# Routing and gathering the first chunk under the second chunk's map, in front of an expert layer

## The chip, the cores and the metric

One NeuronCore of a Trainium2 chip runs the whole kernel as one program. The metric is device time in microseconds (us). TensorE (PE) multiplies, VectorE (DVE), ScalarE (ACT) and GpSimd (POOL) work elementwise, SyncE (SP) starts most loads. Each engine works off its own queue in the order in which the program issues, and waits on semaphores for the others.

## The reference

Two layers on an input of 256 rows and 1024 columns: retention and a dense SwiGLU, then a Fourier mixer and a top-2-of-8 expert SwiGLU, then a last norm. The part that matters here is the end of the Fourier mixer and the start of the experts:

```python
hn = rms_norm(h, mix_norm[1]);  h = h + fourier_mixer(hn, fnet_w_out[0])   # fft2(...).real @ w_out
hn = rms_norm(h, ffn_norm[1]);  h = h + moe_swiglu(hn, ...)
# moe_swiglu:
logits = t @ w_router                                # 256 x 8
top_val, top_idx = lax.top_k(logits, 2)
top_w = softmax(top_val)
gates = sum(one_hot(top_idx, 8) * top_w[..., None], axis=1)
for e in range(8):
    out = out + gates[:, e:e+1] * swiglu(t, w_gate[e], w_up[e], w_down[e])
```

Here t is the normed h, with gain ffn_norm[1]; each expert is 1024 to 3584 and back.

## The kernel before

**Arithmetic.** The large products run in a 32-bit format in three parts (high times high, high times low, low times high), so every operand is split: ScalarE casts the high part (L131 for weights, L253 for data), VectorE subtracts to get the low part (L132, L254). `mm3` (L248 to L250) issues the three products.

**Weights.** `Weights` keeps one list of weight blocks (items) of 1 MB for the whole kernel. Loads go through SyncE's queue (L105) into raw buffers, eleven of them and, for the experts, four more that are lent by tiles that are free then. `split` makes the high and low halves of an item in two pieces each, into one of three slots. `get()` hands out the next item and first issues the splits of up to two items ahead. Before the expert loop, `W.ahead(W.next + W.PARTS - 1)` (L950) issues the splits of the second and third item; that of the first has been issued in the stage before.

**Rows and chunks.** The 256 rows are two chunks of 128 (c). Each row block of X has two halves of 512 columns (hf).

**End of the Fourier mixer.** `out_mm` multiplies by fnet_w_out, six products for one item, chunk and half. Of the four items the first two run for both chunks. The last two, `its`, are done by `close` (L319), quarter by quarter: for chunk c and half hf both items (12 products), then `gained`, in which VectorE adds the accumulator into X (L266) and multiplies by the norm's gain `gb` into a buffer `xgs[hf]` (L267), then the sink of the quarter before.

**Routing.** The sink, `r_sink`, transposes the four 128-column blocks of the gained rows on TensorE (L812), copies them out on ScalarE (`xt`, L813), issues the router products of the quarter before (`r_mm`, L770, four blocks into `lgp[c]`), splits the gained rows into `nh` and `nl`, and sums squares. `route(c)` (L778 to L784) finds the top two of a chunk on VectorE: `o1` marks the first, `mask` both. Then TensorE counts with the matrix `upper` (strictly above the diagonal) how many earlier rows chose the same expert; the count is copied to `pos`. For chunk 1 all rows of chunk 0 are added with `ones`. `gates()` computes the softmax weights on GpSimd into `gts`.

**Gathering.** Experts are handled in pairs by `prep(e0)` (L919). Its first step, `choose`, makes selection maps `pm` on VectorE (L845): for each chunk and expert of the pair a 128 x 128 matrix that has a one where a row sits in a slot. Four steps gather: `gather` multiplies `nh` and `nl` by the maps of both chunks, eight products of 256 columns for one q (L855, L856), and splits the result into `xe`. The last step, `place`, multiplies the maps by `gts` (L872), and VectorE copies the gates and row scales of the pair to `gl` (L874). The first pair runs ahead of the expert loop, except for the last step, which `work.pop(0)()` runs in the loop of the first 512 columns behind the first item's products.

**Experts.** For each expert and each of seven blocks of 512 columns `moe_h` issues 24 gate products (12 for each of two items), ScalarE takes the silu scaled by `RS[e]`, which lies in `gl` (L1103), then `moe_h` issues 24 up products, VectorE multiplies (L1107), and the down products of the block before follow.

The whole stage is issued under `manual_schedule()`: the order of each engine's queue is that of the program text. The tiles of the routing stage lie in pools `pt` and `pc`, those of the experts in pool `pe`.

Of the kernel before, what the change touches and what calls it, by code (L numbers as in the profile page):

```python
# [12 lines left out]
OP = mybir.AluOpType  # L13
PS = bass.MemoryType.PSUM

P = 128
# [10 lines left out]
def cp(c):  # L27
    return slice(c * P, (c + 1) * P)
# [124 lines left out]
def body(nc, tc, a, out, upto=None):  # L153
    with ExitStack() as ctx:
# [75 lines left out]

        def route_consts(rw):
            nc.scalar.dma_start(rw, a["moe_router"][0].rearrange("(k p) e -> p k e", p=P))
            kw = dict(base=0, allow_small_or_imprecise_dtypes=True)
            ge.iota(iota8, pattern=[[1, NE]], channel_multiplier=0, **kw)
            ge.iota(slot, pattern=[[1, P]], channel_multiplier=0, **kw)
            ge.memset(ones, 1.0)

        def acc(i):
            return ps.tile([P, 512], F32, name=f"acc{i}", tag=f"acc{i}")

        def mm(nm="mm"):
            return ps.tile([P, 512], F32, name=nm, tag="mm", bufs=3)
# [9 lines left out]
        def split(hi, lo, src):  # L252
            se.copy(hi, src)  # L253
            ve.tensor_sub(lo, src, hi.bitcast(F32))  # L254
# [3 lines left out]
            se.activation(hi, src, AF.Copy, scale=s)  # L258
            ve.scalar_tensor_tensor(lo, src, s, hi.bitcast(F32), op0=OP.mult, op1=OP.subtract)

        def gained(c, hf, accs=None):


            x = X[:, c, HALF[hf]]
            if accs is not None:
                ve.tensor_add(x, x, accs[2 * c + hf])  # L266
            ve.tensor_mul(xgs[hf], x, gb[:, HALF[hf]])  # L267
            return xgs[hf]

# [6 lines left out]
        def sq_tile():  # L276
            return const.tile([P, 2, 2], F32, name="sq", bufs=2)

        def square(sq, c, hf, src=None):

            se.activation(scr[0], X[:, c, HALF[hf]] if src is None else src, AF.Square, scale=1.0 / 32,  # L281
                          accum_out=sq[:, c, hf:hf + 1])
# [36 lines left out]
        def close(its, accs, sink, early=None):  # L319

            left = None
            for c in range(2):
                for hf in range(2):
                    for i, (it, lh, ll) in enumerate(its):
                        out_mm(accs, it, lh, ll, c, False, i == len(its) - 1, (hf,))
                    xg = gained(c, hf, accs)
                    if early:  # L330
                        early(c, hf)
                    if left:
                        sink(*left)
                    left = (c, hf, xg)
            return lambda: sink(*left)

        def run(hooks, i):
            for f in hooks.get(i, ()):
# [270 lines left out]
        with tc.tile_pool(name="pb", bufs=1) as pb:  # L609
            pb = Aligned(pb)  # L610
            scratch(pb)
            tabr = pb.tile([P, 2, 2 * H1], F32, name="tabr")
            tabd = pb.tile([P, 2, 512], F32, name="tabd", tag="hth", bufs=2)
            accs = [acc(i) for i in range(4)]
            rst, sq = [], sq_tile()

# [23 lines left out]
            for u in range(6):  # L640
                if u:
                    f = hidden(u - 1)
                    hooks = {0: f[:1], 1: f[1:]}
                else:
                    hooks = {1: [left]}
                n = 512 if u < 5 else 256
                g = dense_h(u, hooks)
                if not u:
                    for c in range(2):
                        for hf in range(2):  # L650
                            square(sq, c, hf)
                    rst = [inv_rms(sq, c) for c in range(2)]
                    nc.scalar.dma_start(tabr, a["dft_s"].rearrange("(c p) n -> p c n", p=P))
                    nc.scalar.dma_start(tabd, a["dft_d"].rearrange("(c p) n -> p c n", p=P))
                    gain_bcast(a["mix_norm"][1])
                    route_consts(rw)
                gs = []
                for c in range(2):
                    t = pb.tile([P, 512], F32, name="gs", bufs=3)
                    se.activation(t[:, :n], g[c], AF.Silu, scale=rst[c])  # L660
                    gs.append(t)
                o = dense_h(u)
                if u == 1:
                    split(td[0], td[1], tabd)
                hms[u] = []
                for c in range(2):
                    t = pb.tile([P, 512], F32, name="hm", bufs=3)
                    ve.scalar_tensor_tensor(t[:, :n], o[c], rst[c], gs[c][:, :n], op0=OP.mult, op1=OP.mult)
                    hms[u].append(t)
                if 1 <= u < 5:  # L670
                    for s in range(2):
                        it = W.get()
                        for c in range(2):
                            out_mm(accs, it, *lhs(hT[u - 1], s), c, u == 1 and s == 0, False)
# [26 lines left out]
        with tc.tile_pool(name="pc", bufs=1) as pc:  # L701
# [61 lines left out]

            xt = [pc.tile([P, 8, P], F32, name="xt", tag="fh", bufs=2) for _ in range(2)]
            lgp = [mm("lg") for _ in range(2)]
            sq, late = sq_tile(), []

            def r_mm(c, hf):
                for k in range(4 * hf, 4 * hf + 4):
                    te.matmul(lgp[c][:, :NE], xt[c][:, k], rw[:, k], start=k == 0, stop=k == 7)  # L770
# [35 lines left out]
                ge.tensor_add(gts[:, :, :NE], gts[:, :, :NE], g2)  # L806
                ge.tensor_copy(gts[:, :, NE], rs)

            def r_sink(c, hf, xg):
                p = tr()  # L810
                for k in range(4):
                    te.transpose(p[:, cp(k)], xg[:, cp(k)], ident)  # L812
                se.copy(xt[c][:, 4 * hf:4 * hf + 4], p.rearrange("p (k t) -> p k t", k=4))  # L813
                for ch in late:
                    r_mm(*ch)
                late[:] = [(c, hf)]
                split(nh[:, c, HALF[hf]], nl[:, c, HALF[hf]], xg)
                square(sq, c, hf)

            left = close(its, accs, r_sink)  # L820
            po = mm("po")
            route(0)
            left()
            r_mm(1, 1)
            te.matmul(po[:, 0:8], upper, mask[:, 0], start=True, stop=True)
            route(1)
            ve.tensor_copy(pos[:, 0], po[:, :8])
            te.matmul(po[:, 8:16], ones, mask[:, 0], start=True, stop=False)
            te.matmul(po[:, 8:16], upper, mask[:, 1], start=False, stop=True)
            ve.tensor_copy(pos[:, 1], po[:, 8:16])  # L830
            gates()

        pt_.close()
        if upto == "C":
            return finish()


        with tc.tile_pool(name="pe", bufs=1) as pe, tc.tile_pool(name="dr", bufs=1, space=bass.MemoryType.DRAM) as dr:
            pe = Aligned(pe)
            def choose(e0):  # L840

                pm = pe.tile([P, 2, 2 * P], F32R, name="pm")
                for c in range(2):
                    for j in range(2):
                        ve.tensor_scalar(pm[:, c, cp(j)], slot, pos[:, c, e0 + j:e0 + j + 1],  # L845
                                         mask[:, c, e0 + j:e0 + j + 1], op0=OP.is_equal, op1=OP.mult)
                return pm

            def gather(pm, xe, q, o=None):

                o = o or mm("ga")
                for i in range(2):
                    ds = cp(2 * q + i)
                    for c in range(2):
                        te.matmul(o[:, i * 256:(i + 1) * 256], nh[:, c, ds], pm[:, c], start=c == 0, stop=False)  # L855
                        te.matmul(o[:, i * 256:(i + 1) * 256], nl[:, c, ds], pm[:, c], start=False, stop=c == 1)  # L856
                ov = o.rearrange("p (i j s) -> p j i s", i=2, j=2)
                split(xe[:, :, 0, 2 * q:2 * q + 2], xe[:, :, 1, 2 * q:2 * q + 2], ov)

            def place(pm, last):  # L860

                gl = pe.tile([P, 2, NE + 1], F32, name="gl", bufs=2)
# [56 lines left out]
            def prep(e0):  # L919

                st = {}

                def first():
                    st["pm"] = choose(e0)
                    st["xe"] = pe.tile([P, 2, 2, 8, P], F32R, name="xe", bufs=2)
                    for j in range(2):
                        XE[e0 + j] = st["xe"][:, j]
                yield first
                for q in range(4):
                    yield lambda q=q: gather(st["pm"], st["xe"], q, acc(q) if not e0 else None)  # L930

                def last():
                    gl = place(st["pm"], e0 + 2 == NE)
                    for j in range(2):
                        GT[e0 + j] = gl[:, j, e0 + j:e0 + j + 1]
                        RS[e0 + j] = gl[:, j, NE:]
                yield last
# [147 lines left out]
            for u in range(NU):  # L1085
# [11 lines left out]
                for s, o in enumerate(moe_h(e)):  # L1097
                    if s == 0 and u:
                        hidden_t(u - 1)
                    if s == 0 and not u:  # L1100
                        work.pop(0)()
                hm = pe.tile([P, 512], F32, name="hm")
                se.activation(hm, o, AF.Silu, scale=RS[e])  # L1103
# [95 lines left out]
```

## Time and profile before

| | |
|---|---|
| median of 3 runs | 1424.81 us (1424.56 to 1425.46) |
| profiled execution | 1424.62 us |
| its span | 1422.8 us |
| TensorE busy | 1402.2 us, 99% |
| VectorE busy | 1164.3 us, 82% |
| ScalarE busy | 968.5 us, 68% |
| GpSimd busy | 70.1 us, 5% |
| loads | 437.97 MB, 308 GB/s in the mean |

Times in the profile count from the start of the span; the execution is 1.8 us longer. Busy TensorE is not TensorE at its peak: products overlap, and the time of one in a row (0.39 us for 512 columns) is longer than the distance to the next (0.23 us). So the text goes by the starts of products, and idle time stands in brackets behind a row together with the instruction that ended it. The Fourier mixer's last products begin near 414 us, the experts at 451.41 us.

### The profile page before, as it was taken

The page shows a single profiled execution, that of the slowest core. Times are in us where ns is not written, and L with a number is a line of the kernel's source. Part 1 is how long each engine was busy: PE and PEld are TensorE (multiplying, and loading weights), DVE is VectorE, ACT ScalarE, POOL GpSimd, SP SyncE. Part 2 cuts the span into 40 slices and gives each one's busy share as a digit, 9 for nine tenths or more (in the row PEclk, how much of TensorE's full clock was granted, in tenths as well). Part 3 has the DMA queues.
Part 4 walks back from the last instruction along what each step waited for, and adds up shares of the span by engine and source line. Part 5 has one row for each costly group of instructions (what it writes and reads, how often), then busy time and mean ns, then how long its engine had stood idle before and what let it go on. Part 6 is the DMA issues. An engine that isn't in the chain of part 4 may idle for free. (4 is left out here: it accounts for less than half of the span.)

```text
span 1422.8 us, 17302 instructions
## 1 busy us (share of the span) xinstructions
PE 1402.2 (99%) x6529; PEld 1165.5 (82%) x6529; DVE 1164.3 (82%) x1201; ACT 968.5 (68%) x1118; POOL 70.1 (5%) x109
## 2 busy tenths in 40 slices
PE   8999999999999999999999999999999999999997
PEld 6888878888888888888888888888888888888786
DVE  6866666554577999989899988998898899999996
ACT  5544445444455777777877777787787778778875
POOL 8400000000001000000000000000000000001000
PEclk9999999999999999999999999999999999999999
DMA  8646549755626989999899999999999999999990
GB/s 288 214 155 201 175 142 361 263 183 183 201 101 239 385 327 331 380 350 364 319 380 393 393 353 368 359 351 393 356 395 391 354 381 370 393 373 348 396 375 30
DMA packets 186842, 437.97 MB, mean 308 GB/s; under 512 B 8176, under 2 KB 11008, under 8 KB 186752
## 3 DMA queue, kind: packets, MB, share of 16 engines
q1 hardware_dynamic: 181424, 426.27, 82.0%
q10 hardware_dynamic: 4752, 8.44, 1.6%
q0 software_dynamic: 576, 2.10, 0.4%
q8 instruction: 52, 0.85, 0.2%
q14 instruction: 38, 0.31, 0.1%
HBM read 432.06 MB, written 4.72 MB: 307 GB/s over the span
## 5 line engine op out<-in xcount | busy, mean ns | idle before, releaser
L132 DVE TENSOR_TENSOR wlo<-raw,whi 128x1024 fp32r<-128x1024 f32 (+1 forms) x789 | 923.2, 1218 | 143.8 <-ACT whi L131 140.1
L131 ACT CAST whi<-raw 128x1024 fp32r<-128x1024 f32 (+1 forms) x789 | 786.1, 1047 | 201.5 <-PE acc L250 102.7
L248 PE MATMUL mm<-whi,xe 128*128 128x512 f32 x896 | 354.9, 396 | 0.3 <-PEq L1124 0.3
L250 PE MATMUL mm<-whi,xe 128*128 128x512 f32 x896 | 349.7, 390 | 0.0
L249 PE MATMUL mm<-wlo,xe 128*128 128x512 f32 x896 | 349.3, 390 | 0.0
L249 PE MATMUL acc<-wlo,hth 128*128 128x512 f32 x528 | 205.5, 389 | 0.9 <-DVE wlo L132 0.9
L248 PE MATMUL acc<-whi,hth 128*128 128x512 f32 x528 | 205.7, 390 | 0.0
L250 PE MATMUL acc<-whi,htl 128*128 128x512 f32 x528 | 205.5, 389 | 0.0
L250 PEld LDWEIGHTS mm<-whi,xe 128*128 128x128 f32 x896 | 168.2, 188 | 36.0
L249 PEld LDWEIGHTS mm<-wlo,xe 128*128 128x128 f32 x896 | 168.5, 188 | 33.4 <-DVE wlo L132 0.3
L248 PEld LDWEIGHTS mm<-whi,xe 128*128 128x128 f32 x896 | 168.4, 188 | 33.5 <-issue 0.7
L248 PE MATMUL mm<-whi,nhi 128*128 128x512 f32 (+1 forms) x352 | 135.6, 385 | 0.0
L250 PE MATMUL mm<-whi,nlo 128*128 128x512 f32 (+1 forms) x352 | 133.9, 380 | 0.0
L249 PE MATMUL mm<-wlo,nhi 128*128 128x512 f32 (+1 forms) x352 | 133.7, 380 | 0.0
L249 PEld LDWEIGHTS acc<-wlo,hth 128*128 128x128 f32 x528 | 99.1, 188 | 21.7 <-DVE wlo L132 1.3
L250 PEld LDWEIGHTS acc<-whi,htl 128*128 128x128 f32 x528 | 99.1, 188 | 20.6
L248 PEld LDWEIGHTS acc<-whi,hth 128*128 128x128 f32 x528 | 99.2, 188 | 20.5
L253 ACT CAST hth<-tr 128x512 fp32r<-128x512 f32 (+1 forms) x67 | 38.9, 580 | 81.0 <-PE tr L294 81.0
L250 PEld LDWEIGHTS mm<-whi,nlo 128*128 128x128 f32 x352 | 66.2, 188 | 12.8
L249 PEld LDWEIGHTS mm<-wlo,nhi 128*128 128x128 f32 x352 | 66.3, 188 | 11.9
L248 PEld LDWEIGHTS mm<-whi,nhi 128*128 128x128 f32 x352 | 66.3, 188 | 11.9
L254 DVE TENSOR_TENSOR htl<-tr,hth 128x512 fp32r<-128x512 f32 (+1 forms) x67 | 45.6, 681 | 33.5 <-ACT hth L253 33.5
(288 smaller groups left out, 989.6 us busy)
## 6 DMA issues: line engine op xcount, KB each, us to landing
raw<-in_moe_w_gate SPq DMA_DIRECT2D x110, 1024.0 KB, 7.9
raw<-in_moe_w_down SPq DMA_DIRECT2D x108, 1024.0 KB, 7.8
raw<-in_moe_w_up SPq DMA_DIRECT2D x105, 1024.0 KB, 7.9
raw<-in_ret_w_in SPq DMA_DIRECT2D x23, 1024.0 KB, 5.4
raw<-in_dense_w_gate SPq DMA_DIRECT2D x11, 1024.0 KB, 5.2
raw<-in_dense_w_up SPq DMA_DIRECT2D x11, 1024.0 KB, 8.9
raw<-in_dense_w_down SPq DMA_DIRECT2D x11, 1024.0 KB, 5.8
raw<-in_ret_w_out SPq DMA_DIRECT2D x8, 1024.0 KB, 4.8
```

The costliest lines, as they stand in the source:

```text
L131: self.nc.scalar.copy(hi[sl], t[sl])
L132: self.nc.vector.tensor_sub(lo[sl], t[sl], hi[sl].bitcast(F32))
L248: te.matmul(o, lh, rh, start=first, stop=False)
L249: te.matmul(o, lh, rl, start=False, stop=False)
L250: te.matmul(o, ll, rh, start=False, stop=last)
L253: se.copy(hi, src)
L254: ve.tensor_sub(lo, src, hi.bitcast(F32))
```

## The change

The routing stage is written out in place of `close`. Chunk 0's transposes, router products, top two, positions and first maps are issued between chunk 1's map products. Transposes now read X itself: the norm's gain is multiplied into the router's weights `rw` instead, in the dense layer's fourth block (a load of the gain as 8 x 128, a transpose, a multiplication). The gathers of the first pair are issued chunk by chunk, 16 products for chunk 0 (12 behind chunk 1's last router products and 4 behind the position products) and 16 for chunk 1. The maps for them are in a tile `pm0` of the routing stage's pool, and the splits into `xe` follow in the experts' pool; the last step of the first pair makes the maps once more in the experts' pool. `warm(n)` issues n products of 512 columns that nobody reads. The step `place` of the first pair moves from behind the first 12 gate products to behind all 24. The experts' pool is opened with `reuse_waits="tile"`, so that a tile waits for those that lay in its place, and not for the whole pool before.

```diff
         def route_consts(rw):
             nc.scalar.dma_start(rw, a["moe_router"][0].rearrange("(k p) e -> p k e", p=P))
+            nc.scalar.dma_start(rg[:8], a["ffn_norm"][1].rearrange("(k p) -> k p", p=P))
...
+        def choose(pm, e0, c):
+            for j in range(2):
+                ve.tensor_scalar(pm[:, c, cp(j)], slot, pos[:, c, e0 + j:e0 + j + 1],
+                                 mask[:, c, e0 + j:e0 + j + 1], op0=OP.is_equal, op1=OP.mult)
+
+        def gather(o, pm, q, c):
+            for i in range(2):
+                ds = cp(2 * q + i)
+                te.matmul(o[:, i * 256:(i + 1) * 256], nh[:, c, ds], pm[:, c], start=not c and not i, stop=False)
+                te.matmul(o[:, i * 256:(i + 1) * 256], nl[:, c, ds], pm[:, c], start=False, stop=bool(c and i))
...
+                if u == 3:
+                    p = tr()
+                    te.transpose(p[:, :8], rg[:8], ident[:8, :8])
+                    ve.tensor_mul(rw, rw, p[:, :8, None].to_broadcast([P, 8, NE]))
...
+            def maps(c, hf, i):
+                it, lh, ll = its[i]
+                out_mm(accs, it, lh, ll, c, False, i == 1, (hf,))
+            def r_t(c, hf):
+                p = tr()
+                for k in range(4):
+                    te.transpose(p[:, cp(k)], X[:, c, cp(4 * hf + k)], ident)
+                se.copy(xt[c][:, 4 * hf:4 * hf + 4], p.rearrange("p (k t) -> p k t", k=4))
+            def hi(c, hf):
+                se.copy(nh[:, c, HALF[hf]], xgs[hf])
+            def lo(c, hf):
+                ve.tensor_sub(nl[:, c, HALF[hf]], xgs[hf], nh[:, c, HALF[hf]].bitcast(F32))
+            def warm(n):
+                o = mm("warm")
+                for _ in range(n):
+                    te.matmul(o, nh[:, 0, :P], nh[:, 0, HALF[0]], start=True, stop=True)
-            left = close(its, accs, r_sink)
-            po = mm("po")
+            for hf in range(2):
+                maps(0, hf, 0)
+                if hf:
+                    r_t(0, 0)
+                    hi(0, 0)
+                    lo(0, 0)
+                    square(sq, 0, 0)
+                maps(0, hf, 1)
+                gained(0, hf, accs)
+            maps(1, 0, 0)
+            r_t(0, 1)
+            hi(0, 1)
+            lo(0, 1)
+            square(sq, 0, 1)
+            r_mm(0, 0)
+            maps(1, 0, 1)
+            r_mm(0, 1)
+            gained(1, 0, accs)
             route(0)
-            left()
+            maps(1, 1, 0)
+            r_t(1, 0)
+            hi(1, 0)
+            square(sq, 1, 0)
+            maps(1, 1, 1)
+            x = X[:, 1, HALF[1]]
+            ve.tensor_add(x, x, accs[3])
+            po, pm = mm("po"), pt.tile([P, 2, 2 * P], F32R, name="pm0", tag="tdh")
+            te.matmul(po[:, 0:8], upper, mask[:, 0], start=True, stop=True)
+            r_mm(1, 0)
+            ve.tensor_copy(pos[:, 0], po[:, :8])
+            choose(pm, 0, 0)
+            r_t(1, 1)
+            square(sq, 1, 1)
+            ve.tensor_mul(xgs[1], x, gb[:, HALF[1]])
+            hi(1, 1)
+            lo(1, 0)
+            warm(3)
+            go = [acc(q) for q in range(4)]
             r_mm(1, 1)
-            te.matmul(po[:, 0:8], upper, mask[:, 0], start=True, stop=True)
+            for q in range(3):
+                gather(go[q], pm, q, 0)
             route(1)
-            ve.tensor_copy(pos[:, 0], po[:, :8])
-            te.matmul(po[:, 8:16], ones, mask[:, 0], start=True, stop=False)
-            te.matmul(po[:, 8:16], upper, mask[:, 1], start=False, stop=True)
-            ve.tensor_copy(pos[:, 1], po[:, 8:16])
+            po = tr()
+            te.matmul(po[:, 0:8], ones, mask[:, 0], start=True, stop=False)
+            te.matmul(po[:, 0:8], upper, mask[:, 1], start=False, stop=True)
+            gather(go[3], pm, 3, 0)
+            ve.tensor_copy(pos[:, 1], po[:, :8])
+            choose(pm, 0, 1)
             gates()
+            warm(2)
+            lo(1, 1)
+            for q in range(4):
+                gather(go[q], pm, q, 1)
...
-        with tc.tile_pool(name="pe", bufs=1) as pe, ...
+        with tc.tile_pool(name="pe", bufs=1, reuse_waits="tile") as pe, ...
...
+                def maps():
+                    st["pm"] = pe.tile([P, 2, 2 * P], F32R, name="pm")
+                    for c in range(2):
+                        choose(st["pm"], e0, c)
                 def first():
-                    st["pm"] = choose(e0)
+                    if e0:
+                        maps()
...
+                def part(q):
+                    o = mm("ga") if e0 else go[q]
+                    for c in range(2) if e0 else ():
+                        gather(o, st["pm"], q, c)
+                    ov, xe = o.rearrange("p (i j s) -> p j i s", i=2, j=2), st["xe"]
+                    split(xe[:, :, 0, 2 * q:2 * q + 2], xe[:, :, 1, 2 * q:2 * q + 2], ov)
                 for q in range(4):
-                    yield lambda q=q: gather(st["pm"], st["xe"], q, acc(q) if not e0 else None)
+                    yield lambda q=q: part(q)
                 def last():
+                    if not e0:
+                        maps()
                     gl = place(st["pm"], e0 + 2 == NE)
...
                 for s, o in enumerate(moe_h(e)):
                     if s == 0 and u:
                         hidden_t(u - 1)
-                    if s == 0 and not u:
+                    if s == 1 and not u:
                         work.pop(0)()
```

## Rows read from the trace of the kernel before

**Rows 1.** The page, part 1: busy time, share and instructions of each engine.

```profile
PE 1402.2 (99%) x6529; PEld 1165.5 (82%) x6529; DVE 1164.3 (82%) x1201; ACT 968.5 (68%) x1118; POOL 70.1 (5%) x109
```

**Rows 2.** Waits (us in total, times, longest): PE, whole span; DVE, 452 to 1395.

```profile
PE po L828 <- DVE pos L827: 1.4, 1, 1.4
...
DVE wlo L132 <- DMA raw<-in_moe_w_down: 0.6, 2, 0.4
```

**Rows 3.** Windows: stretch, length, busy PE, PEld, DVE, ACT, POOL, clock, DMA share, GB/s.

```profile
442.00:443.50 1.50, 0.09 (x1) 0.09 (x1) 1.18 (x8) 0.00 (x0) 1.25 (x5) 1.00 0.00 0
...
444.00:450.00 6.00, 5.10 (x25) 5.04 (x25) 2.36 (x7) 1.18 (x2) 5.15 (x22) 0.50 0.73 262
...
1415.00:1419.00 4.00, 0.21 (x1) 0.00 (x0) 2.61 (x6) 2.88 (x7) 1.14 (x2) 1.00 0.16 61
...
1419.00:1421.00 2.00, 0.00 (x0) 0.00 (x0) 0.00 (x0) 0.00 (x0) 0.00 (x0) 0.72 1.03 380
```

**Rows 4.** Timeline (start, us, what) of PE, 424 to 452: chunk maps to last gather.

```profile
424.94 0.39 PE L248 MATMUL acc<-whi,yh 128*128 128x512 f32 x1
...
430.38 0.60 PE L812 MATMUL tr<-ident,gx 128*128 128x128 f32 x4
...
430.73 0.47 PE L248 MATMUL acc<-whi,yh 128*128 128x512 f32 x1
...
434.00 0.96 PE L770 MATMUL lg<-rw,xt 128*128 128x8 f32 x8
...
434.82 0.48 PE L248 MATMUL acc<-whi,yh 128*128 128x512 f32 x1
...
445.13 0.55 PE L855 MATMUL acc<-pm,nhi 128*128 128x256 f32 x1 [0.90 <-DVE pm L845]
...
451.29 0.28 PE L856 MATMUL acc<-pm,nlo 128*128 128x256 f32 x1
```

**Rows 5.** Timeline of DVE, the same stretch.

```profile
428.50 0.68 DVE L266 TENSOR_TENSOR X<-X,acc 128x512 f32<-128x512 f32 x1
...
430.58 0.69 DVE L266 TENSOR_TENSOR X<-X,acc 128x512 f32<-128x512 f32 x1 [0.67 <-PE acc L250]
...
441.91 0.16 DVE L778 COPY lgt<-lg 128x8 f32<-128x8 f32 x1
...
443.06 0.23 DVE L784 SCALAR_TENSOR_TENSOR mask<-iota,if,o 128x8 f32<-128x8 f32 x1
...
444.38 1.12 DVE L845 TENSOR_SCALAR pm<-slot,pos,mask 128x128 fp32r<-128x128 f32 x4
```

**Rows 6.** Timeline of ACT, the same stretch and the start of the experts.

```profile
431.01 0.59 ACT L813 COPY xt<-tr 128x512 f32<-128x512 f32 x1 [3.87 <-PE tr L812]
...
451.61 0.59 ACT L253 CAST xe<-acc 128x512 fp32r<-128x512 f32 x1 [0.37 <-PE acc L856]
...
452.09 5.80 ACT L131 CAST whi<-raw 128x1024 fp32r<-128x1024 f32 x6
```

**Rows 7.** Timeline of PE at the start of the experts, 451 to 476.

```profile
451.41 0.40 PE L248 MATMUL mm<-whi,xe 128*128 128x512 f32 x1
...
454.16 0.95 PE L872 MATMUL acc<-gts,pm 128*128 128x9 f32 x8
...
454.97 0.49 PE L248 MATMUL mm<-whi,xe 128*128 128x512 f32 x1
...
457.83 0.39 PE L248 MATMUL mm<-whi,xe 128*128 128x512 f32 x1
```

**Rows 8.** Timeline of DVE at the start of the experts.

```profile
452.23 0.69 DVE L254 TENSOR_TENSOR xe<-acc,xe 128x512 fp32r<-128x512 f32 x1 [0.27 <-ACT xe L253]
...
453.18 4.63 DVE L132 TENSOR_TENSOR wlo<-raw,whi 128x1024 fp32r<-128x1024 f32 x4 [0.26 <-ACT whi L131]
...
457.73 0.17 DVE L874 COPY gl<-acc 128x18 f32<-128x18 f32 x1
...
457.81 6.89 DVE L132 TENSOR_TENSOR wlo<-raw,whi 128x1024 fp32r<-128x1024 f32 x6
```

More of the change, by code (lines that the diff above doesn't have):

```diff
@@ L259, in split_s, with gained @@
             ve.scalar_tensor_tensor(lo, src, s, hi.bitcast(F32), op0=OP.mult, op1=OP.subtract)
-        def gained(c, hf, accs=None):
+        def gained(c, hf, accs):
             x = X[:, c, HALF[hf]]
-            if accs is not None:
-                ve.tensor_add(x, x, accs[2 * c + hf])
+            ve.tensor_add(x, x, accs[2 * c + hf])
             ve.tensor_mul(xgs[hf], x, gb[:, HALF[hf]])
@@ L613, in body @@
             tabd = pb.tile([P, 2, 512], F32, name="tabd", tag="hth", bufs=2)
+            rg = pb.tile([P, P], F32, name="rg")
             accs = [acc(i) for i in range(4)]
@@ L765, in body @@
             lgp = [mm("lg") for _ in range(2)]
-            sq, late = sq_tile(), []
+            sq = sq_tile()
             def r_mm(c, hf):
@@ L807, in gates @@
                 ge.tensor_copy(gts[:, :, NE], rs)
-            def r_sink(c, hf, xg):
+            def maps(c, hf, i):
+                it, lh, ll = its[i]
+                out_mm(accs, it, lh, ll, c, False, i == 1, (hf,))
+            def r_t(c, hf):
                 p = tr()
                 for k in range(4):
-                    te.transpose(p[:, cp(k)], xg[:, cp(k)], ident)
+                    te.transpose(p[:, cp(k)], X[:, c, cp(4 * hf + k)], ident)
                 se.copy(xt[c][:, 4 * hf:4 * hf + 4], p.rearrange("p (k t) -> p k t", k=4))
[L814 to L818, printed above, removed]
@@ L835, in body @@
             return finish()
-        with tc.tile_pool(name="pe", bufs=1) as pe, tc.tile_pool(name="dr", bufs=1, space=bass.MemoryType.DRAM) as dr:
+        with tc.tile_pool(name="pe", bufs=1, reuse_waits="tile") as pe, tc.tile_pool(name="dr", bufs=1, space=bass.MemoryType.DRAM) as dr:
             pe = Aligned(pe)
[L840 to L858, printed above, removed]
             def place(pm, last):
```

## The prediction

> **What bounds the kernel now.** I read the page's first part first: TensorE is busy for 1402.2 of 1422.8 us [rows 1]. So the question for any change is which microseconds TensorE waits or runs slowly, and the other engines matter only where it waits for them. Next the waits: TensorE has one of over a microsecond between routing and experts, the 1.4 us for `pos` of chunk 0, and another 0.9 us for the first selection map `pm` ([rows 2], first row; [rows 4], the row of 445.13, in brackets). Through 943 us of experts VectorE waits 0.6 us for loads of weights, so loads limit nothing there [rows 2]. Third, the granted clock: 1.00 in 442 to 443.5 and 0.50 in 444 to 450, which is the lower level, 1.2 GHz [rows 3]. The engine had run narrow router products (8 columns) and then waited. The 32 gathering products take from 445.13 to 451.41, 6.28 us; those at the end, at full clock, start 0.12 us apart, so that 32 would take 3.8 [rows 4, 7].
>
> The stage that the change touches runs from the last map product (start of chunk 0's at 424.94, all 48 of both chunks with what is put between them until about 437.65) to the first expert product at 451.41: 13.8 us for transposes, router, top two, positions, maps and gathers. The last part is what stands at the other end: VectorE's queue at the start of the experts [rows 8], which sets when weights are ready.
>
> **The routed stage, step by step.** All times are put on the clock of the profiled execution.
> 24 map products take from 424.94 to 430.38 [rows 4], so a block of six takes 1.36. Four transposes take 0.35 (430.38 to 430.73), and the product behind them 0.08 more than another (0.47 to 0.39). Eight router products take 0.82 (434.00 to 434.82). ScalarE's copy of transposes begins 0.63 after they begin (430.38 to 431.01) and takes 0.59; VectorE's addition into X begins 0.2 after the block's end and takes 0.69 [rows 4 to 6].
> Chunk 0: two blocks end at 427.66, one of the second half at 429.02. The transposes of X wait for the addition of 428.50, done at 429.18 [rows 5]: 0.2 lost. Then block (431.0), block of chunk 1 (432.4), transposes of the second half, router products, block (435.0), router products (435.9), block (437.3), transposes, block: the last map product is issued until 439.1. That is 1.4 later than now, because transposes and router products of chunk 0 and half of chunk 1 stand ahead of it. Chunk 0's top two (441.91 to 443.29 now, 1.38 us [rows 5]) run on VectorE from 436.6, behind the addition and the multiplication of chunk 1's first half (from 435.25, 0.69 each), to 438.0, beside map products, at no cost; if they came late, the first thing behind them would be the position product at 439.1, with 1.1 us to spare.
> After 439.1: X of the last quarter is ready at 440.0, under the position product and eight router products (until 440.3). Transposes until 440.65; copy at 440.93, done at 441.5; three unread products of 0.23 fill this wait and end at 441.4. Router products until 442.4; top two of chunk 1 from 442.55 to 443.93. Under it lie the first 12 gathers of chunk 0, 12 x 0.12 = 1.44. VectorE writes chunk 0's two maps earlier, in 440.1 to 440.7: four take 1.12 [rows 5], two 0.56. The position products of chunk 1 end at 444.3, `pos` and two maps at 445.1; four gathers and two unread products (0.48 + 0.45) fill that. Sixteen gathers of 0.12 are left: the experts begin at 447.1 instead of 451.41. **Gain so far 4.3 us**, of which 2.4 is the clock on the gathers (6.28 - 3.84), which rests on the clock staying at its upper level; the rest is chunk 0's share of the tail.
>
> **The start of the experts.** Here the change moves a step, and adds to it. The product that places gates (L872, 8 instructions, 0.81 us) now stands behind the first 12 gate products, at 454.16, and needs maps that have long been made [rows 7]. Afterwards it stands behind 24, and VectorE must make the four maps a second time just ahead of it, in a new tile. VectorE works in the order in which the program issues: the row shows four low halves of weights, then `gl`, then six [rows 8], exactly the program's order with the step behind 12 products. Behind 24, `W.get()` for the second half of the gate's weights has issued two more. So six low halves stand ahead of the four maps.
> Now: the last gather ends at 451.41, the first low half begins at 453.18, 1.77 later (ScalarE's copy of the gather at 451.61, its cast of weights at 452.09 [rows 6]). Afterwards four gathers end 0.48 apart, closer than VectorE's 0.6 per subtraction, so take 1.9: the first low half begins at 449.0. Six take 6.9 (457.81, 6.89 us [rows 8]): 455.9. The maps take 1.12: the first is there at 456.2, the third at 456.75, the last at 457.0. TensorE has done its 24 gate products by 447.1 + 2 x 2.75 (451.41 to 454.16) + about 0.2 for the first low half of the second weights = 452.8. **It then waits 3.4 us for the map**, and places by 457.6. Now the first product of the other matrix (up) starts at 457.83 [rows 7]. So of 4.3 us gained, 4.1 are given back: 0.2 are left.
> Nothing later returns them. The low halves of the weights behind are ready (two items are split by then), loads are ahead, and TensorE has no wait of note in the rest. The gates' own chain on GpSimd starts from the last square and the top two, which come no later than now, and the placing product reads it later than now.
>
> **The other edits.** Norm weights into the router's: one small load on ScalarE's queue, one transpose (of four, 0.60; a quarter to all of it, 0.15 to 0.6, and I take 0.1 since it overlaps the next) and one VectorE multiplication of 64 columns, under dense products, where VectorE has room (82% busy over the span [rows 1]); without that cover it would be at most one row of 0.69. Waits by tile for the new pool let the extra weight buffers load earlier: between 0 and the 0.6 us that VectorE waits for loads [rows 2]; I take 0, as those buffers are needed tens of microseconds later. The five unread products cost 5 x 0.23 = 1.1 if no wait covers them; by the steps above each lies in a wait. Sum: 1424.62 (the profiled execution, span 1422.8 and 1.8 around it) - 4.3 + 4.1 + 0.1 = **1424.5 us**. The median of before is 1424.81, 0.2 above that execution. The handshakes of the steps may be off by 0.8 together: 1423.6 to 1425.4.
>
> **The clock during the new wait.** Rows bear on it from both sides. At the kernel's end TensorE idles from 1415.2 and the clock is still 1.00 in 1415 to 1419, then falls within 1419 to 1421; at the routing it was down in 444 to 450 after a wait of 1.4 us behind narrow products [rows 3]. A wait of 3.4 behind wide products lies between these. I take that it holds, by the row of the end, where the products ahead were wide too. The Trainium skill (TensorE: Matmul & The Clock Gate, section "What's actually happening") says that the reduced clock is the default state and that activity is what releases the array from it; by that rule this wait speaks against the change, and the time would be that of the first rival.
>
> **Rivals.**
> First, the clock falls in the wait for the map. For it: the row of 444 to 450. Price by that row: 5.10 us of TensorE work at half clock, so 2.55 lost: 1427.1 (1425.5 if it returns sooner).
> Second, slower: the clock falls already in the routing. Its place is the stretch of narrow products, waits and short fills from 439.1 to 443.9, and it decides if TensorE is at 1.2 GHz when chunk 0 is gathered. Then 12 gathers lose 0.1 each (24 of the 32 of before at half speed: 6.28 less 8 x 0.12 is 5.3, 0.22 each) beyond the top two that hide them now, +1.2; the fourth group with its two unread products +0.9; 16 gathers +1.6. The experts begin 3.7 later, VectorE's queue with them: 1428.2. Against: eight transposes and three wide products are in the stretch, and the wait of before with nothing in it is gone.
> Third, faster: the wait for the map is not there, because the second maps are made ahead of the low halves, or their waits don't tie them: all 4.1 us stay: 1420.4. Against: [rows 8] has VectorE in program order to the instruction. For it: only that I read the order from the code.
> That the change doesn't shorten the routing at all (maps of chunk 1 delayed by chunk 0's work) I count within the second.
>
> **Chances.** Forecast 0.45, clock in the wait 0.27, clock in the routing 0.13, no wait 0.15. What a measurement can tell from no change is 0.2%, 2.8 us: faster ends at 1421.8, slower begins at 1427.5. Faster is the third rival, 0.15; slower the second and a small part of the first, 0.15; the rest 0.70. The range goes from 1420.4, the middle of the third, to 1427.9, which takes in nearly all of the first and some of the second.
>
> **What would show it.** Of the changed kernel: the first expert product near 447, gathers 0.12 apart, granted clock 1.00 through 440 to 447 (else the second rival); the placing product (L872's successor) with about 3.4 us of idle time ended by VectorE's `pm`, behind six low halves in VectorE's row (else the third); the clock in and after that wait (first rival); the first up product within 0.8 of 457.6. The prediction is wrong if that placing product doesn't wait, or if the wait is there and the experts' end isn't moved by it.

## The result and the profile after

The changed kernel takes 1434.14 us (median of 4 runs, 1432.98 to 1435.7) beside 1424.68 us of the kernel before: slower, ratio 1.0067, 95% interval 1.0056 to 1.0079. It lies 6 us above the stated range. The profiled execution took 1432.98 us with a span of 1431.2, 8.4 more than before; it was the fastest of the four, so what follows accounts for 8.4 us, and not for the 9.5 between the medians.

The page's first line for the engines of the changed kernel shows TensorE busy for 3.9 us more than [rows 1]; the unread products and stretches of low clock are in that. The span grew by 8.4, so more than half of the loss is waiting.

```profile
PE 1406.1 (98%) x6535; PEld 1165.7 (81%) x6535; DVE 1165.4 (81%) x1206; ACT 968.4 (68%) x1118; POOL 74.1 (5%) x109
```

**The loss is in two places, and the larger is 220 us ahead of the routing.** The timeline of ScalarE in the changed kernel, first block of the dense layer (ACTq is the engine's issue of a load, the instruction that starts it; columns as in [rows 6]):

```profile
226.59 0.44 ACTq L232 DMA_DIRECT2D rw<-in_moe_router  x1
...
227.07 4.90 ACTq L233 DMA_DIRECT2D rg<-in_ffn_norm  x1
...
232.08 1.27 ACT L674 ACTIVATE gs<-mm,rs 128x512 f32<-128x512 f32 x2 [6.24 <-issue]
```

The same stretch before:

```profile
226.53 0.45 ACTq L232 DMA_DIRECT2D rw<-in_moe_router  x1
...
227.07 1.27 ACT L660 ACTIVATE gs<-mm,rs 128x512 f32<-128x512 f32 x2 [1.29 <-POOL rs L287]
```

Before, the silu (`gs`) follows the issue of the router's weights at once. Afterwards the 4 KB load of the gain (`rg`) stands between them, and its issue holds the engine from 227.07 to 231.97, 4.90 us, where the issue ahead of it took 0.44. The silu starts 5.0 later. TensorE needs the buffer that the silu reads, as its timeline in the changed kernel shows:

```profile
228.24 0.39 PE L251 MATMUL mm<-whi,nlo 128*128 128x512 f32 x1
...
232.82 0.50 PE L249 MATMUL mm<-whi,nhi 128*128 128x512 f32 x1 [4.19 <-ACT gs L674]
...
233.47 0.63 PE L251 MATMUL mm<-whi,nlo 128*128 128x512 f32 x1
...
236.46 0.50 PE L249 MATMUL mm<-whi,nhi 128*128 128x512 f32 x1
...
245.46 0.60 PE L294 MATMUL tr<-ident,hm 128*128 128x128 f32 x4
```

The last product ahead of the wait starts at 228.24 and the next at 232.82: 4.58 apart where 0.23 is usual, so 4.35 lost. From 233.47 they run 0.43 apart, at half clock, until 236.46. The transposes behind them start at 245.46; before, in this row of TensorE's timeline:

```profile
239.31 0.60 PE L294 MATMUL tr<-ident,hm 128*128 128x128 f32 x4
```

That is 6.15 later; 0.05 of it was there before the wait. The transpose of the gain in the fourth block adds 0.42, as TensorE's next group of transposes shows, in the changed kernel and before:

```profile
346.70 0.60 PE L294 MATMUL tr<-ident,hm 128*128 128x128 f32 x4
```

```profile
340.13 0.60 PE L294 MATMUL tr<-ident,hm 128*128 128x128 f32 x4
```

So the routing starts 6.57 late.

**The routing and the start of the experts.** TensorE of the changed kernel, from the last gather on; its rows answer to [rows 4, 7]:

```profile
454.04 0.28 PE L348 MATMUL acc<-pm,nlo 128*128 128x256 f32 x1
...
454.16 0.40 PE L249 MATMUL mm<-whi,xe 128*128 128x512 f32 x1
...
459.70 0.39 PE L251 MATMUL mm<-whi,xe 128*128 128x512 f32 x1
...
463.42 1.26 PE L923 MATMUL acc<-gts,pm 128*128 128x9 f32 x8 [3.34 <-DVE pm L340]
...
464.53 0.48 PE L249 MATMUL mm<-whi,xe 128*128 128x512 f32 x1
...
465.31 0.56 PE L249 MATMUL mm<-whi,xe 128*128 128x512 f32 x1
...
468.95 0.40 PE L249 MATMUL mm<-whi,xe 128*128 128x512 f32 x1
```

The gathers end 0.12 apart, at full clock, and the experts start at 454.16: 2.75 later than before, so 3.82 of the 6.57 are won in the routing. Then the 24 gate products end by 459.93 (the last starts at 459.70, and 0.23 is the distance to the next), and the placing product (L923) waits until 463.42 for its map. The first up product is at 464.53, 6.70 later than before: all 3.82 are gone, and 0.13 more. Behind the wait nine products take 3.64 (465.31 to 468.95) where 2.07 is usual: 1.6 at low clock. Sum: 6.57 + 0.13 + 1.6 = 8.3, of the 8.4 in the span. VectorE in the same stretch, to be read beside [rows 8]:

```profile
453.60 2.48 DVE L255 TENSOR_TENSOR xe<-acc,xe 128x512 fp32r<-128x512 f32 x4 [0.91 <-ACT xe L254]
...
456.01 7.01 DVE L132 TENSOR_TENSOR wlo<-raw,whi 128x1024 fp32r<-128x1024 f32 x6
...
462.94 1.10 DVE L340 TENSOR_SCALAR pm<-slot,pos,mask 128x128 fp32r<-128x128 f32 x4
...
464.72 0.18 DVE L925 COPY gl<-acc 128x18 f32<-128x18 f32 x1 [0.67 <-PE acc L923]
```

Six low halves from 456.01, then the four maps at 462.94, then the gates. The placing product can only start behind the first map.

### The profile page after: what moved, and what is told of

It reads as the page before. It is cut to its first block, busy times and chain, and to the rows that moved or that the text cites. A ratio compares the mean times of both kernels' runs of the same rounds, so it can differ in the third digit from the quotient of the medians.

```text
span 1431.2 us, 17314 instructions
## 1 busy us (share of the span) xinstructions
PE 1406.1 (98%) x6535; PEld 1165.7 (81%) x6535; DVE 1165.4 (81%) x1206; ACT 968.4 (68%) x1118; POOL 74.1 (5%) x109
```

## The experiments

All are timed against the kernel before, run beside them: 1424.47 us beside e1 to e4 (27 runs, 1423.94 to 1425.4), 1424.46 beside e5 to e8 (33 runs, 1423.77 to 1425.36), and 1424.55 beside e9 and e10 (one run).

**e1: the load of the gain issued two blocks later.**

```diff
-            nc.scalar.dma_start(rg[:8], a["ffn_norm"][1]...)      # in route_consts, behind four loads
...
+                if u == 2:
+                    nc.scalar.dma_start(rg[:8], a["ffn_norm"][1]...)
```

> The changed kernel, with the 4 KB load of the norm's gain (rg) issued in the dense layer's third block instead of behind four other loads on ScalarE's queue in the first. Theory: its issue held ScalarE 4.90 us (issues beside it 0.4), TensorE waited 4.36 us between two products for the silu behind it and ran 1.7 us longer at 1.2 GHz; all 6.1 us go, 1434.1 becomes 1428.0, and the stage of the routing keeps its 2.3 us of loss: the wait for the second maps (3.5) and the clock behind it (1.7) are still there. Rival: ScalarE stood still there for the silu's own reason (row scales, buffers), and moving the load moves nothing: 1434 again.

Measured: 1427.02 (1426.84 to 1428.48), ratio to before 1.0020, interval 1.0011 to 1.0029. The wait of 4.2 us for the silu is gone; the longest wait of TensorE in this kernel is now the one at the experts (us in total, times, longest):

```profile
PE acc L924 <- DVE pm L339: 3.3, 1, 3.3
```

7.1 us come back between the medians, 1 more than worked out; the rival falls. The clock behind the wait for the maps differs from execution to execution: it was low for 3.4 us in the profile of the changed kernel and for 6.8 in this one, whose execution took 1428.29. The stretches of this one (columns as in [rows 3]):

```profile
453.00:457.00 4.00, 0.93 (x5) 0.42 (x3) 4.00 (x5) 1.55 (x2) 2.84 (x4) 1.00 1.05 409
457.00:464.00 7.00, 6.74 (x20) 5.71 (x21) 3.42 (x7) 2.56 (x3) 0.00 (x0) 0.52 1.03 397
```

While TensorE waits (busy 0.93 of 4.00 us) the clock is at 1.00; it is low in the stretch behind, where the products run again. So sums of under 1.5 us between these kernels are not resolved by one profile.

**e2: the load alone, in the kernel before.**

```diff
             nc.scalar.dma_start(rw, a["moe_router"][0]...)
+            nc.scalar.dma_start(rg[:8], a["ffn_norm"][1]...)      # read by nobody
```

> The kernel before, with nothing of the change but the 4 KB load of the norm's gain as the fifth load in a row on ScalarE's queue, into a tile that nobody reads. Theory: the issue alone costs TensorE 4.4 us of waiting and 1.7 us of low clock: 1424.7 becomes 1430.8, with the shift complete before 245 us. Rival: the other memory layout of the dense stage or the routing's edits have a part in the loss before 430 us, and the load alone costs under 1 us: 1425.

Measured: 1430.23 (1429.61 to 1431.78), ratio 1.0045, interval 1.0032 to 1.0059. ScalarE's timeline has the same issue, 4.84 long, and the silu behind it:

```profile
227.08 4.84 ACTq L233 DMA_DIRECT2D rg<-in_ffn_norm  x1
...
232.03 1.27 ACT L662 ACTIVATE gs<-mm,rs 128x512 f32<-128x512 f32 x2 [6.18 <-issue]
```

One load of 4 KB, with no reader, costs 5.8 us; the rival by which it costs under 1 us, and the layout or the routing the rest, falls. The tile `rg` that the load needs is in e4 too, which loses nothing.

**e4: five loads with few pieces.** A piece is one run of bytes that lie side by side in memory; a load is made of as many pieces as it has such runs. This is the kernel before, with the router's load moved away and two unread loads of the gain in its place.

```diff
-            nc.scalar.dma_start(rw, a["moe_router"][0]...)        # 1024 pieces of 32 B; now at u == 2
+            nc.scalar.dma_start(rg[:8], a["ffn_norm"][1]...)      # 8 pieces of 512 B
+            nc.scalar.dma_start(rg[8:16], a["ffn_norm"][1]...)
```

> The kernel before, where the router's weights (1024 pieces of 32 B) are loaded two blocks later, and two unread loads of the gain, 8 pieces each, stand behind the three others: again five loads in a row on ScalarE's queue, but 400 pieces where it was over 1600. If the number of loads under way holds up the fifth issue, ScalarE stands still for some 5 us and the time is 1430.8, as with the gain alone. If it is the number of pieces, the fifth issue takes 0.4 us and the time is 1424.7 to 1425.

Measured: 1424.23 (1423.74 to 1425.49), ratio 1.0000, interval 0.9991 to 1.0010. The fourth and the fifth issue and the silu:

```profile
226.57 0.35 ACTq L232 DMA_DIRECT2D rg<-in_ffn_norm  x1
...
226.95 0.29 ACTq L233 DMA_DIRECT2D rg<-in_ffn_norm  x1
...
227.35 1.27 ACT L662 ACTIVATE gs<-mm,rs 128x512 f32<-128x512 f32 x2 [1.53 <-POOL ones L237]
```

Five loads in a row are no obstacle: the fifth takes 0.29. So it is the pieces of the router's load that hold the next one. (The count in the expectation is too low. The three loads ahead have 640 pieces, 256 of 1032 B, 256 of 2048 B and 128 of 4096 B, so the five here have 656, where the five of the changed kernel have 1672.)

**e5: the two last loads exchanged.** The question left was whether the queue is full or the pieces are being made.

```diff
+            nc.scalar.dma_start(rg[:8], a["ffn_norm"][1]...)
             nc.scalar.dma_start(rw, a["moe_router"][0]...)
-            nc.scalar.dma_start(rg[:8], a["ffn_norm"][1]...)
```

> The changed kernel with the last two of the five loads exchanged: the gain (8 pieces) fourth, the router's weights (1024 pieces) fifth, on ScalarE's queue. Theory A, room: the queue holds some 1660 pieces and an issue waits until its own fit in; the total is the same, so the router's load is held instead and ScalarE stands still as long: 1434. Theory B, work: the pieces of the router's load are made for some 5 us after its issue, and only the next issue on the queue feels it; with nothing behind it ScalarE goes on, and the time is that of e1_gain_later, 1427.

Measured: 1427.68 (1426.9 to 1428.43), ratio 1.0021, interval 1.0012 to 1.0030, as e1. The same five loads, and none of the issues is long:

```profile
226.60 0.35 ACTq L232 DMA_DIRECT2D rg<-in_ffn_norm  x1
...
226.99 0.40 ACTq L233 DMA_DIRECT2D rw<-in_moe_router  x1
...
227.49 1.27 ACT L674 ACTIVATE gs<-mm,rs 128x512 f32<-128x512 f32 x2 [1.64 <-POOL ones L237]
```

The total of pieces is the same as in the changed kernel, so theory A falls: the load with 1024 pieces doesn't wait until its own fit in. It is issued in 0.40 and ScalarE goes on; only the load issued right behind it, in the changed kernel and in e2, waits. That the queue works at the pieces for some 5 us after the issue (theory B) fits these runs. So does a limit on what may be pending when an issue starts: 1664 pieces stood ahead of the held one, 648 ahead of the fifth here and in e4, and no run lies between. What the queue does in that time no trace shows.

**e3: the second maps earlier.** On top of e1, the maps are issued between the low halves of the second and the third item.

```diff
-                def last():
-                    if not e0:
-                        maps()
+                if not e0:
+                    yield maps
+                def last():
...
-            W.ahead(W.next + W.PARTS - 1)
+            W.ahead(W.next + 1)
+            work[-2]()                                            # the maps
+            W.ahead(W.next + W.PARTS - 1)
```

> As e1_gain_later, and the second maps of the first pair are issued on VectorE between the low halves of the second and third expert weights instead of behind the fourth. Theory: the placing product finds its maps and waits for nothing, the clock stays at 2.4 GHz, and the 3.8 us by which the experts start earlier are kept but for the transpose of the gain (0.4): 1421.4, 3.3 under before. Rival: the weights come 1.1 us later instead, and TensorE waits for the third item's low half about as long as it waited for the maps: over 1425.

Measured: 1423.64 (1423.25 to 1423.74), ratio 0.9994, interval 0.9985 to 1.0003: not told from before, 3.4 better than e1, 2.2 short of what I expected. The placing product waits no more and the clock stays at its upper level to the end of the experts. The timelines of VectorE and, below it, ScalarE show what was missed:

```profile
452.17 1.11 DVE L339 TENSOR_SCALAR pm<-slot,pos,mask 128x128 fp32r<-128x128 f32 x4
...
453.19 4.62 DVE L132 TENSOR_TENSOR wlo<-raw,whi 128x1024 fp32r<-128x1024 f32 x4
...
457.74 0.17 DVE L926 COPY gl<-acc 128x18 f32<-128x18 f32 x1
...
459.59 4.63 DVE L132 TENSOR_TENSOR wlo<-raw,whi 128x1024 fp32r<-128x1024 f32 x4 [1.69 <-ACT whi L131]
```

```profile
457.94 0.69 ACT L1173 ACTIVATE hm<-mm,gl 128x512 f32<-128x512 f32 x1 [3.36 <-DVE gl L926]
```

The maps are out of the way at 453.2, but the copy of the gates (`gl`) now stands behind two low halves, the maps and four more low halves, at 457.74. The silu (`hm`) needs it, ScalarE's casts stand behind the silu, and VectorE stands idle for 1.69 ahead of its next low half. TensorE pays most of it here (us in total, times, longest) and another 0.3 in a wait for a later low half:

```profile
PE tr L293 <- DVE hm L1177: 1.3, 1, 1.3
```

The theory overlooked the gates. The rival was wrong too: the time is under its 1425, and it was not the third item that came late but what hangs on the gates.

**e6: the first maps kept.** On top of e1; nothing is made twice, and the placing product is back where it stood.

```diff
+        pm0 = const.tile([P, 2, 2 * P], F32R, name="pm0")         # the experts' maps use it too
...
-                    y = pc.tile([P, 2, S], F32, name="y", bufs=2)
+                    y = pc.tile([P, 2, S], F32, name="y")         # makes room
...
                 def last():
                     if not e0:
-                        maps()
+                        st["pm"] = pm0
...
-                    if s == 1 and not u:
+                    if s == 0 and not u:
```

> As e1_gain_later, but the first pair's maps stay in one tile from the routing stage on (one buffer fewer in the Fourier stage makes room), so nothing is made twice, and the placing product is back behind the first 12 gate products, with the copy of the gates ahead of the third item's successors on VectorE. Theory: in e3_maps_early the copy stood behind two more low halves, so the silu, ScalarE's casts and then TensorE came 1.7 us late; here nothing waits and the 3.4 us by which the experts start earlier are kept: 1421.3 to 1421.8. Rival: VectorE's backlog of weights at the start of the experts is the bound whatever the place of the maps, and the time is that of e3_maps_early, 1423.6.

Measured: 1421.43 (1421.28 to 1421.64, 11 runs), ratio 0.9978, interval 0.9969 to 0.9987. This is faster than both kernels and as the theory said; the rival's 1423.6 falls. TensorE and, below it, VectorE at the start of the experts:

```profile
448.35 0.40 PE L248 MATMUL mm<-whi,xe 128*128 128x512 f32 x1
...
451.09 0.95 PE L925 MATMUL acc<-gts,pm 128*128 128x9 f32 x8
...
451.90 0.49 PE L248 MATMUL mm<-whi,xe 128*128 128x512 f32 x1
```

```profile
450.19 4.69 DVE L132 TENSOR_TENSOR wlo<-raw,whi 128x1024 fp32r<-128x1024 f32 x4
...
454.80 0.17 DVE L927 COPY gl<-acc 128x18 f32<-128x18 f32 x1
```

The experts start at 448.35, 3.06 earlier than before; the placing product stands 2.74 behind that, without a wait, and the next gate product 3.55 behind it, where before it was 3.56 [rows 7]. The copy of the gates stands behind four low halves as before [rows 8]. The 3.06 is kept: the medians differ by 3.03. The edit keeps the maps and also moves the placing product back; no run takes the two apart.

**e7: the gain turned at the kernel's start.** On top of e6.

```diff
+        nc.scalar.dma_start(gr[8:16], a["ffn_norm"][1]...)
...
-            te.transpose(p[:, :8], gr[:8], ident[:8, :8])
+            te.transpose(p[:, :16], gr[:16], ident[:16, :16])
...
+            ve.tensor_copy(ones[:, :8], p[:, 8:16])                # kept there until rw is multiplied
```

> As e6_first_maps_kept, and the gain for the router is loaded with the first gain at the kernel's start and turned by the same transpose (16 rows instead of 8), so that the transpose in the dense layer (0.42 us between two products) and its load are gone. Theory: 0.4 us less than e6_first_maps_kept. Rival: the transpose hid a wait that was there anyway, or the second load at the start delays the first products by 0.3 to 0.5: no difference.

Measured: 1421.34 (1421.06 to 1421.66), ratio 0.9977, interval 0.9968 to 0.9986: no difference from e6. The first wait of TensorE, for this load, is 4.7 us instead of 2.3 in e6, and by 225 us ScalarE is 0.35 later than in e6 (its load of the tables at 225.52 and 225.17), which is about what the transpose cost. So the rival was right in that the second load at the start takes back what the transpose gave.

```profile
PE g L407 <- DMA gx<-in_ffn_norm: 4.7, 1, 4.7
```

**e8, e9, e10: without the unread products.** e7 with both calls of `warm` taken out, three times.

```diff
-            warm(3)
...
-            warm(2)
```

> As e7_gain_at_start without the five unread products. Theory: without them the stretch of narrow products and waits looks to the clock as it did in the kernel before, it falls to 1.2 GHz ahead of the gathers, and 2 to 3.5 us are lost. Rival: the transposes, the map products and the gathers of chunk 0 keep it at 2.4 GHz, and the time is the same or, by what the products push aside, up to 0.4 us less.

Measured: 1422.3 (1420.96 to 1424.03), ratio 0.9984, interval 0.9975 to 0.9993. Neither theory fits as written: five of the eleven runs lie from 1420.96 to 1421.43, six from 1422.3 to 1424.03, while those of e6 and e7 stay within 0.6. The profile was one of the lower five, clock 1.00 throughout. Two more profiles tell the groups apart.

> The same kernel as e8_no_unread, for another profile: its eleven times lay in two groups, 1421.0 to 1421.4 and 1422.3 to 1424.0, and the profile was of the first, with the clock at 2.4 GHz through the routing. Theory: in executions of the second group the clock falls in the routing or behind it, so that a time over 1422 comes with a stretch of granted clock 0.5 between 440 and 455 us that ends over 3 us later. Rival: the spread has another cause (loads, launch), and a time over 1422 comes with the clock at 1.0 there.

> As e9_no_unread_again, a third profile of the same kernel, with the same two expectations: a time over 1422 with a stretch of granted clock 0.5 between 440 and 455 us, or without.

e9 took 1422.98, e10 1421.48. The same windows of both (stretch, length, busy PE, PEld, DVE, ACT, POOL, clock, DMA share, GB/s), e9:

```profile
440.00:443.00 3.00, 2.33 (x21) 2.05 (x19) 2.57 (x6) 1.83 (x7) 0.00 (x0) 1.00 0.45 119
443.00:446.00 3.00, 3.00 (x18) 3.00 (x18) 1.21 (x7) 0.58 (x2) 2.43 (x8) 0.59 1.05 405
```

and e10:

```profile
440.00:443.00 3.00, 2.32 (x21) 2.04 (x20) 2.57 (x6) 1.83 (x7) 0.00 (x0) 1.00 0.51 128
443.00:446.00 3.00, 2.96 (x25) 2.75 (x24) 1.74 (x10) 0.51 (x2) 2.49 (x8) 1.00 1.06 409
```

The slower execution has the clock down in the second window, the faster has not, though TensorE was busy alike in the first (2.33 and 2.32 us). So the theory of e9 holds for these two, and the rival by which loads or the launch spread the times is not needed. That the slow runs of e8 have the same cause is read from their times alone. With it, what the unread products buy is that the clock holds in all 22 runs of e6 and e7 instead of in about half.

## Why the prediction was wrong

**The step that failed** is in "The other edits": "one small load on ScalarE's queue ... under dense products, where VectorE has room". I priced what the load feeds (a transpose, a multiplication) and not its issue, which stands on ScalarE right behind a load of 1024 pieces and right ahead of a silu whose buffer TensorE waits for. In the sum it stood at nothing; it costs 5.8 us alone (e2), and without its wait the kernel takes 1427.0 or 1427.7 (e1, e5), inside the range. I had the list of issues and did not ask which instruction stands behind each of them: the row above for before shows the silu starting as soon as the last issue is done. There was little slack: the silu came 4.95 later against the products ahead of it, and TensorE lost 4.35, so about 0.6 was covered. The Trainium skill (DMA: Bandwidth & Descriptors, section "Anatomy of one DMA — SWDGE (gpsimd) path") says, of the path that GpSimd issues on, that one can emit many descriptors before the added cost shows. No run here issues such a load from GpSimd. On ScalarE's queue the issue itself behaves alike (0.40 to 0.52 us for 1024 pieces); the next issue does not, at 4.84 and 4.90.

**The routed stage** was forecast to start the experts 4.3 earlier; it was 3.8, counted from TensorE's late start of the stage. The mechanism held: gathers 0.12 apart at full clock, chunk 0's top two beside map products.

**The wait for the second maps** came where the prediction put it: 3.5 us from the last gate product's end where 3.4 was worked out, behind six low halves, and the net for the first up product was +0.13 where -0.2 was forecast. Both kernels that take the cause away bear it out: with the maps earlier (e3) or kept (e6) the wait is gone.

**The clock in that wait** went the way of the first rival: in all three profiles that have the wait (the changed kernel, e1, e5) the clock is low behind it, for 3.4, 6.8 and 3.4 us. I had weighed it at 0.27 against 0.45. The row of the kernel's end, where TensorE idles for over 4 us at full clock, was read too far: in the wait itself the clock held here too (1.00 in 453 to 457 of e1), and it was low behind it, when the products ran again. At the kernel's end no products follow that could have shown this. The price of 2.55 was taken from a longer stretch; 1.6 was measured where the stretch was 3.4 us. The transpose cost 0.42, where I put 0.1. That e1's 1427.0 lies so close to that rival's 1427.1 is partly luck: the rival has one term of 2.55, e1 has 0.42, 0.13 and 1.6 or more, by the execution.

**The second rival** (clock down in the routing) didn't come in the profiles of the changed kernel, e6 and e7, nor, as their times lie within 0.6 us, in any of the 22 runs of e6 and e7; e9 shows that without the unread products it can. **The third** (no wait for the maps) was wrong as the order of the queues said. Of the waits by tile for the experts' pool no run separates a cost or a gain; it was not tried alone.

## What to carry to other kernels

A load is an instruction of the engine that issues it: for each added or moved one, write down what is issued ahead of it on that queue, how many pieces that has, and which instruction stands behind it, before asking what the load feeds. Where a step is moved, list the queue it moves into by program order: the maps that were made a second time stood behind six instructions of 1.15 us, and keeping the first ones, with the placing product back in its old place, was worth 5.6 us (e1 to e6). Where loads stand in a row on one queue, put that of many small pieces last, as e5 does.

## What the runs showed of the hardware

On ScalarE's queue a load of 1024 pieces of 32 B was issued in 0.40 to 0.52 us, but a load of only 8 pieces issued right behind it took 4.84 and 4.90 us (e2, the changed kernel); behind another load of 8 pieces the same load took 0.29 (e4). A lone transpose of an 8 x 128 tile between wide products cost 0.42 us, about what four full transposes cost (0.35, and 0.08 in the product behind them [rows 4]). With the same program the granted clock fell in one execution and not in the next (e9, e10), which is worth 1.5 us there: with waits of about 0.7 and 0.3 us among narrow products it fell in some executions, and with five unread products in these waits in none that the times or profiles show. Behind a wait of 3.3 us the clock was low in all three profiles that have one, though in the wait itself it was still at its upper level (e1).
